# A fused decoder layer: output weights and one group of down weights split earlier, stored in HBM and read back

## The chip, the cores and the metric

The kernel runs on one core of a Trainium2 chip. Its engines are TensorE (PE, matmuls; PEld is its weight load), VectorE (DVE), ScalarE (ACT), GpSimd (POOL) and SyncE (SP, which here only issues DMAs). Each engine works through its own queue in order, and waits on semaphores for the others. SP, ACT and POOL each issue DMAs. SBUF holds the working tiles, PSUM the eight banks into which matmuls accumulate, and HBM the rest.

The metric is the device time of one execution in microseconds, as the median over runs.

## The reference

One step of a decoder layer on 1024 prompt tokens and 64 decode tokens (8 sequences of 8), all in float32. An RMS norm and one input projection feed two mixers, retention (8 heads) and sliding-window attention (8 query heads, 2 key/value heads). Their outputs are concatenated, projected by `w_out`, and added to the input; a squared-ReLU MLP of four times the width follows.

```python
hn = rms_norm(x, norm_mix_gain)
proj = hn @ w_in
...
o_r = rms_norm(o_r).reshape(b, t, RET_WIDTH) * jax.nn.silu(g_r)
...
h = x + jnp.concatenate([o_r, o_s], axis=-1) @ w_out
hf = rms_norm(h, norm_ffn_gain)
h = h + jnp.square(jax.nn.relu(hf @ w_up)) @ w_down
return h, new_ret, new_k, new_v
```

Here x has 1088 rows of 1024, `w_out` is 1024 x 1024, `w_up` 1024 x 4096 and `w_down` 4096 x 1024.

## The kernel before

**Split products.** Every large product is made of three matmuls in a fast float32 form (`mm3`, L174 to L177). Each operand is the sum of a high part, which is the value cast to that form, and a low part, which is what the cast left out; the three products are high x high, low x high and high x low. So each weight and each activation has to be split before use: one cast on ACT (L791) and one subtraction on DVE (L792), together `halve`. `wsplit` (L794) does that for a weight tile of 128 x 512, giving a tile of 128 x 2 x 512 (high and low). In `wload` (L66), for the input projection, the same is done at L80 and L82.

**The front** (L86 to L529). x is loaded and normalised, and the first two blocks of q columns are projected for the window attention (`proj_q`, L265). The loop at L307 then goes over nine token tiles, `proj_tok` giving k and v of the window attention, with a short chain over ACT, DVE and POOL for each tile. Before this loop its weights `wkv` are loaded; the second q block's weights `wq1` are loaded after it (L341). Then eight blocks of window attention follow (`swa_block`, L378). Their scores are in tiles of tag "s" (three buffers of 128 x 4 x 256) and their transposed probabilities in tiles of tag "pt" (two buffers of 128 x 2 x 512). PE fills the gaps of that chain with projections for retention.

**Retention and output projection** (L509 to L1089). The output projection starts while retention still runs: `out_early` for the first half of the tokens (s = 0), then `out_parts` for the second (s = 1). For each s, each pair of feature blocks m and each mixer ("a" attention, "r" retention), `wo_pair` (L819) loads half rows of two blocks of `w_out` into a raw tile and splits them in two `wsplit`s. So each half of each block of `w_out` is loaded and split twice, once for each s: 16 loads and 32 splits.

**Up** (L1098 to L1200). Sixteen blocks `up(fp)` of 256 hidden columns each. The product is done by a Strassen-like scheme with seven products in place of eight quarter products; the activations' combinations are in `ops`, and `left` (L1036) gives the seven weight tiles of a block one by one: some straight from the raw quarters (products 1, 2, 4), the others from sums on POOL (`comb`). The squared results go to HBM as `u_d`, seven combinations for each block. `first_down` loads and splits operands of the first products of down while the last block runs.

**Down** (L1206 to L1276). The sixteen blocks f are taken in five groups of 2, 4, 4, 4 and 2; in each group the seven products in the order `DOWN` = 1, 6, 7, 4, 5, 3, 2. For a product i of a group, each f's weight tile comes from its generator `left` (L1236), the activations `ur` are loaded from `u_d` (L1246) and split (`uh`, `ul`, L1248), and PE accumulates over f into eight banks (4 row blocks m, 2 halves s). A result is copied out of its bank by ACT the first time (L1264, `copied`) and added by DVE afterwards (L1267, `added`). New banks are taken at products 1, 5 and 2. Weight tiles have the tags "wa" and "wb", four buffers each.

**Order.** The program gives an order of emission; a planner with a timing model then sets the order of each engine's queue. `tc.issue_after(x)` puts what is emitted under it behind instruction x. Buffers of a tag go round: a tile waits until the last reader of the buffer's previous tile is done.

Of the kernel before, what the change touches and what calls it, by code (L numbers as in the profile page):

```python
# [11 lines left out]
F32 = mybir.dt.float32  # L12
F32R = mybir.dt.float32r
AF = mybir.ActivationFunctionType
ALU = mybir.AluOpType
# [5 lines left out]
P = 128  # L21
# [15 lines left out]
def hymba_layer(ctx: ExitStack, tc: tile.TileContext, a: dict, o: dict):  # L37
    nc = tc.nc
# [22 lines left out]
    def cload(name):  # L61
        t_ = const.tile(list(a[name].shape), F32, name="c_" + name)
        nc.sync.dma_start(t_, a[name])
        return t_

    def wload(src, kk, name, lo_eng="p", parts=2, after=()):  # L66
        hi = ring.tile([P, 2048], F32R, tag="whi", name=name + "_hi")
        lo = ring.tile([P, 2048], F32R, tag="wlo", name=name + "_lo")
        n = 2048 // parts
        after = list(after)  # L70
        for h in range(2):
            raw = ring.tile([P, 1024], F32, tag="raw", name=f"{name}_raw{h}", bufs=3)
            for q in range(0, 1024, n):
                nc.sync.dma_start(raw[:, q : q + n], src[:, h * 1024 + q : h * 1024 + q + n])
                if after:
                    load_x(*after.pop(0))
            for q in range(0, 1024, n):
                h_, l_ = (v[:, h * 1024 + q : h * 1024 + q + n] for v in (hi, lo))
                r_ = raw[:, q : q + n]
                nc.scalar.copy(h_, r_)  # L80
                eng = nc.vector if lo_eng[(2 * h + q // n) % len(lo_eng)] == "v" else nc.gpsimd
                eng.tensor_tensor(l_, r_, h_.bitcast(F32), ALU.subtract)  # L82
        return hi.rearrange("p (k n) -> p k n", k=kk), lo.rearrange("p (k n) -> p k n", k=kk)
# [44 lines left out]
    g_d = scratch.tile([P, 4, T], F32, name="g_d")  # L128
    ms_hi_d = scratch.tile([P, 4, T], F32, name="ms_hi_d")
    ms_lo_d = scratch.tile([P, 4, T], F32, name="ms_lo_d")  # L130
    y_d = scratch.tile([P, 4, 4, 2, Q], F32, name="y_d")
    u_d = [scratch.tile([P, 2, 2, 7, Q], F32, name=f"u_d{g}") for g in range(8)]

    def rsqrt_inplace(ap, n):
# [168 lines left out]
    spread(rst, rsb)  # L303


    w = wload(a["w_in"][2], 8, "wkv", "v")
    for t in range(9):  # L307
        off, c, r0 = tok_tile(t)
        rt = rst[:, t : t + 1]
        ps = proj_tok(t, w, psA.tile([P, 512], F32, tag="mm", name="pst"))  # L310
        sq = sp.tile([P, 128], F32, tag="hsq", name="hsq")
        nc.scalar.activation(sq, ps[:, :128], AF.Square, scale=rt)
        r = sp.tile([P, 2], F32, tag="hr", name="hr")
        nc.vector.tensor_reduce(r, sq.rearrange("p (h d) -> p h d", h=2), AX.X, ALU.add)
        nc.vector.tensor_scalar(r, r, 1.0 / 64.0, EPS, ALU.mult, ALU.add)
        rsqrt_inplace(r, 2)
        nc.vector.tensor_scalar(r, r, rt, None, ALU.mult)
        kn = sp.tile([P, 128], F32, tag="kn", name="kn")
        nc.vector.tensor_tensor(
            kn.rearrange("p (h d) -> p h d", h=2), ps[:, :128].rearrange("p (h d) -> p h d", h=2),  # L320
            r.unsqueeze(2).broadcast_to([P, 2, 64]), ALU.mult,
        )
        pt = psB.tile([P, 512], F32, tag="t2", name="ptk")[:, :128]
        nc.tensor.transpose(pt, kn, ident)
        if t < 8:
            cols = slice(t * 128, t * 128 + 128)
            for kv in range(2):
                p_ = slice(kv * 64, kv * 64 + 64)
                for d_ in (p_, slice(64 - kv * 64, 128 - kv * 64)):
                    nc.scalar.activation(kh2[kv][d_, cols], pt[p_], AF.Copy, scale=qkg[p_, 1:2])  # L330
                    nc.vector.scalar_tensor_tensor(
                        kl2[kv][d_, cols], pt[p_], qkg[p_, 1:2], kh2[kv][p_, cols].bitcast(F32), ALU.mult, ALU.subtract
                    )
            nc.vector.tensor_scalar(vs[:, t, :], ps[:, 128:256], rt, None, ALU.mult)
        if t == 7:
            nc.vector.tensor_scalar(k8[:, 0:128], pt, qkg[:, 1:2], None, ALU.mult)
        if t == 8:
            nc.vector.tensor_scalar(k8[:, 128:192], pt[:, 64:128], qkg[:, 1:2], None, ALU.mult)
            nc.vector.tensor_scalar(v8, ps[64:128, 128:256], rt[64:128], None, ALU.mult)

    proj_q(1, wload(a["w_in"][1], 8, "wq1", "v"))  # L341
    nc.sync.dma_start(o["kp"], k8[:, 0:128])
    nc.sync.dma_start(o["vp"], vs[:, 7, :])
    nc.sync.dma_start(o["kc"][:, :, 120:128], k8[:, 128:192].rearrange("p (b i) -> p b i", b=8))
# [473 lines left out]

    def wo_pair(s, m, half):  # L819

        raw = mw.tile([P, 1024], F32, tag="raw", name=f"wo{half}{s}_{m}_raw", bufs=3)
        c0 = 512 * (half == "a")
        nc.sync.dma_start(
            raw.rearrange("p (m n) -> p m n", m=2), a["w_out"][m : m + 2, :, c0 : c0 + 512].rearrange("m p n -> p m n")
        )
        for i in range(2):
            yield wsplit(raw[:, i * 512 : i * 512 + 512], "wa", f"wo{half}{s}_{m + i}", nc.vector)

    def out_half(s, half, ps, h, w, first, last):
        for k in range(4):  # L830
# [113 lines left out]
    qbh, qbl, kh, kl = split_space([ring.tile([P, 1024], F32R, tag="raw", name=f"qk{i}", bufs=3) for i in range(3)])  # L944
    for i, x in enumerate("hl"):
        mix[0, "r" + x] = slot(6 + i, F32R, "mixr" + x)[:, : 8 * Q].rearrange("p (k h n) -> p k h n", k=4, h=2)
    held, mxr, mxrx = {}, None, ExitStack()
    for t in range(5):
        if t == 0:
            for _ in range(2):  # L950
# [82 lines left out]
                for x in "hl"  # L1033
            ]

    def left(order, src, name, lo_eng, raw_tag="raw", raw_pool=None, s_tag="S", s_pool=None, tags=("wa", "wb"), raws=None, sums=None):  # L1036

        r1, r2 = raws or (
            rawload(src[:, i * 1024 : i * 1024 + 1024], f"{name}_r{i + 1}", raw_tag, raw_pool) for i in range(2)
# [8 lines left out]
        for n, i in enumerate(order):  # L1048
            if i in (5, 6) and 5 not in have:
                comb(5, a21, a22, ALU.add)  # L1050
                comb(6, have[5], a11, ALU.subtract)
            if i == 7:
                comb(7, a11, a21, ALU.subtract)
            if i == 3:
                comb(3, a12, have[6], ALU.subtract)
            yield wsplit(have[i], tags[n % len(tags)], f"{name}_w{i}", lo_eng)

    late = lambda: bank("pso")
# [137 lines left out]
        return lambda: halve(u_hi, u_lo, u_raw, nc.vector)  # L1196

    split6 = []
    for fp in range(16):
        up(fp)  # L1200
    opx.close()
    ux.close()

# [19 lines left out]
    for g, (f0, nf) in enumerate(((0, 2), (2, 4), (6, 4), (10, 4), (14, 2))):  # L1223
        gens = []
        for f in range(nf):
            own = ("rawb", dn, "Sb", dn) if f else ("raw", mw, "S", mid)
            gens.append(left(
                DOWN, a["w_down"][f0 + f], f"wd{f0 + f}", nc.vector, *own, tags=("wb" if f % 2 else "wa",),
                raws=raws1 if (g, f) == (0, 1) else None, sums=sums1 if (g, f) == (0, 1) else None))
        banks = {}  # L1230
        for i in DOWN:
            ws = []
            for f, gen in enumerate(gens):
                behind = copied[(6, 6, 7, 4)[f] if g == 1 else 4] if g in (1, 2) and i == 1 else None
                with tc.issue_after(behind) if behind else ExitStack():
                    ws.append(next(gen))  # L1236
            if g == 0 and i in begun:
# [6 lines left out]
            for f in () if g == 0 and i in begun else range(0, nf, 2):  # L1244
                if g or i in (3, 2):
                    nc.sync.dma_start(ur[:, f : f + 2], u_d[(f0 + f) // 2][:, :, :, RIGHT[i], :])  # L1246
                with tc.issue_after(copied[{4: 6, 5: 7}[i]]) if g == 0 and i in (4, 5) else ExitStack():
                    halve(uu[0][:, f : f + 2], uu[1][:, f : f + 2], ur[:, f : f + 2], nc.vector)  # L1248
            q_ = INTO[i]
            if q_ not in accs:  # L1250
                accs[q_] = dn.tile([P, 4, 2, Q], F32, tag=f"a{q_}", name=f"a{q_}")
# [147 lines left out]
```

## Time and profile before

| | us |
|---|---|
| median of 3 runs | 1189.44 |
| lowest, highest | 1187.9, 1189.73 |
| profiled execution | 1188.43 |
| its span | 1186.7 |

The page of the profile gives, for the span, the busy shares of the engines, the span in 40 slices, the DMA queues, the chain that ended last and the costliest groups of instructions. Of the chain, 81% is on PE, 6% on DVE, 5% on DMA, 3% on issue and 2% each on ACT and POOL. The granted clock of PE was full throughout. DMAs moved 169.44 MB, 143 GB/s in the mean.

| stage, by the first and last start of its matmuls | from, us |
|---|---|
| k and v of the window attention (`pst<-wkv`) | 31.9 to 73.3 |
| v of retention (`pst<-wv`) | 285.5 to 367.5 |
| output projection (`pso`) | 373.1 to 489.9 |

How to read it: a group of instructions has its line, engine, operation and tiles, then its count, its busy time and the mean length of one, and last how long its engine had stood idle just before, and for whom. The line is often that of a helper, so the tiles tell the stage. A matmul's end is modelled and the next one starts before it, so PE can show no idle time where it starts fewer matmuls than it could.

### The profile page before, as it was taken

How to read it: one execution, taken by the hardware profiler on the slowest of the kernel's cores; microseconds unless marked ns; L12 is line 12 of the kernel's file. 1: busy time of each engine (PE TensorE's matmuls, PEld its weight loads, DVE VectorE, ACT ScalarE, POOL GpSimd, SP SyncE). 2: the span in 40 equal slices, each digit the busy share in tenths (PEclk: the TensorE clock that was granted, in tenths of full speed). 3: DMA queues.
4: the chain of work that ended last, by engine and by line, in shares of the span. 5: the costliest groups of instructions: out<-in, count | busy, mean ns of one | idle time of the engine just before them, and what ended most of it. 6: DMA issues, size and time to landing. Idle time of an engine off the chain costs nothing.

```text
span 1186.7 us, 23488 instructions
## 1 busy us (share of the span) xinstructions
PE 1169.6 (99%) x9405; PEld 1123.5 (95%) x9405; DVE 839.1 (71%) x1546; ACT 513.8 (43%) x1055; POOL 494.2 (42%) x393
## 2 busy tenths in 40 slices
PE   8999999999999999999999999999999999999998
PEld 7999988989778899999999999999989999999998
DVE  7556868632257769887766667666788787888676
ACT  8343544553334347644444444444642333333231
POOL 0125333332255542467666666566383142053000
PEclk9999999999999999999999999999999999999999
DMA  7221235333525555343444434444685456443225
GB/s 247 73 62 68 93 102 166 104 115 98 180 74 168 181 183 156 113 156 133 141 151 148 144 130 141 151 148 157 236 290 157 148 169 203 143 155 104 76 59 187
DMA packets 102277, 169.44 MB, mean 143 GB/s; under 512 B 12000, under 2 KB 68256, under 8 KB 101912
## 3 DMA queue, kind: packets, MB, share of 16 engines
q1 hardware_dynamic: 88807, 123.80, 31.5%
q10 hardware_dynamic: 10800, 35.23, 9.3%
q0 software_dynamic: 2560, 8.91, 2.3%
q8 instruction: 74, 1.21, 0.4%
q14 instruction: 36, 0.29, 0.1%
HBM read 114.30 MB, written 53.61 MB: 142 GB/s over the span
## 4 chain that ended last, share of the span: by engine, by line
PE 81%; DVE 6%; DMA 5%; issue 3%; ACT 2%; POOL 2%; SPq 0%; ACTq 0%; DVEq 0%; POOLq 0%
PE psd L176 9%; PE psd L177 9%; PE psd L175 9%; PE psx L175 5%; PE psx L177 5%; PE psx L176 5%; PE psz L175 2%; PE psz L177 2%; PE psz L176 2%; PE pst L175 2%; PE pst L176 2%; PE pst L177 2%; PE psf L175 2%; PE psf L177 2%; PE psf L176 2%
## 5 line engine op out<-in xcount | busy, mean ns | idle before, releaser
L175 PE MATMUL psd<-uh,wd_w 128*128 128x272 f32 x896 | 258.4, 288 | 3.2 <-DVE a L1267 2.4
L176 PE MATMUL psd<-uh,wd_w 128*128 128x272 f32 x896 | 259.3, 289 | 0.0
L177 PE MATMUL psd<-ul,wd_w 128*128 128x272 f32 x896 | 257.9, 288 | 0.7 <-DVE ul L792 0.7
L175 PEld LDWEIGHTS psd<-uh,wd_w 128*128 128x128 f32 x896 | 169.1, 189 | 4.3 <-DVE a L1267 3.4
L177 PEld LDWEIGHTS psd<-ul,wd_w 128*128 128x128 f32 x896 | 168.7, 188 | 0.9 <-DVE ul L792 0.9
L176 PEld LDWEIGHTS psd<-uh,wd_w 128*128 128x128 f32 x896 | 168.4, 188 | 0.0
L1267 DVE TENSOR_TENSOR a<-a,psd 128x272 f32<-128x272 f32 x248 | 101.9, 432 | 48.9 <-PE psd L177 48.8
L792 DVE TENSOR_TENSOR wu_w<-wu_s,wu_w 128x512 fp32r<-128x512 f32 x64 | 61.9, 971 | 49.8 <-ACT wu_w L791 49.2
L791 ACT CAST wd_w<-wd_s 128x512 fp32r<-128x512 f32 x64 | 37.5, 621 | 119.0 <-PE psd L177 107.2
L792 DVE TENSOR_TENSOR ul<-ur,uh 128x1088 fp32r<-128x1088 f32 x56 | 84.0, 1527 | 4.1 <-ACT uh L791 4.1
L1120 DVE SCALAR_TENSOR_TENSOR m<-m,rsf 128x272 f32<-128x272 f32 x96 | 72.9, 760 | 3.2 <-ACT rsf L914 0.5
L175 PE MATMUL psx<-op_1h,wu_w 128*128 128x272 f32 x256 | 74.3, 290 | 0.4 <-ACT m L1136 0.4
L177 PE MATMUL psx<-op_1l,wu_w 128*128 128x272 f32 x256 | 74.1, 289 | 0.0
L175 PE MATMUL psx<-op_0h,wu_w 128*128 128x272 f32 x256 | 74.1, 290 | 0.0
L177 PE MATMUL psx<-op_0l,wu_w 128*128 128x272 f32 x256 | 74.1, 289 | 0.0
L176 PE MATMUL psx<-op_1h,wu_w 128*128 128x272 f32 x256 | 73.7, 288 | 0.0
L176 PE MATMUL psx<-op_0h,wu_w 128*128 128x272 f32 x256 | 73.7, 288 | 0.0
L365 POOL TENSOR_TENSOR sp<-sp,ssp 128x1024 f32<-128x1024 f32 (+1 forms) x16 | 28.6, 1787 | 88.4 <-DVE ssp L364 60.1
L791 ACT CAST uh<-ur 128x1088 fp32r<-128x1088 f32 x56 | 59.7, 1101 | 12.7 <-PE psd L176 9.1
L175 PE MATMUL psf<-hnh,wqk_hi 128*128 128x384 f32 (+1 forms) x192 | 63.5, 331 | 0.2 <-DVE qkst L517 0.2
L177 PE MATMUL psf<-hnl,wqk_hi 128*128 128x384 f32 (+1 forms) x192 | 63.2, 329 | 0.0
L176 PE MATMUL psf<-hnh,wqk_lo 128*128 128x384 f32 (+1 forms) x192 | 62.8, 327 | 0.0
(343 smaller groups left out, 3619.4 us busy)
## 6 DMA issues: line engine op xcount, KB each, us to landing
ur<-u_d SPq DMA_DIRECT2D x53, 544.0 KB, 5.2
u_d<-r4t SPq DMA_DIRECT2D x32, 544.0 KB, 4.6
wu_r<-in_w_up ACTq DMA_DIRECT2D x32, 512.0 KB, 4.4
wd_r<-in_w_down ACTq DMA_DIRECT2D x30, 512.0 KB, 6.5
u_d<-r3t SPq DMA_DIRECT2D x32, 408.0 KB, 2.9
y<-in_xY POOLq DMA_DIRECT2D x16, 272.0 KB, 3.5
y_d<-y POOLq DMA_DIRECT2D x16, 272.0 KB, 3.2
yt<-y_d SPq DMA_DIRECT2D x16, 272.0 KB, 2.9
```

Source lines behind the costliest of these rows:

```text
L175: nc.tensor.matmul(ps, lh, rh, start=first, stop=False, skip_group_check=more)
L176: nc.tensor.matmul(ps, ll, rh, start=False, stop=False, skip_group_check=more)
L177: return nc.tensor.matmul(ps, lh, rl, start=False, stop=last, skip_group_check=more)
L365: nc.gpsimd.tensor_tensor(s, s, ss.unsqueeze(2).broadcast_to([P, 4, n]), ALU.mult)
L791: nc.scalar.copy(hi, src)
L792: lo_eng.tensor_tensor(lo, src, hi.bitcast(F32), ALU.subtract)
L1120: nc.vector.scalar_tensor_tensor(t_, src, 0.0, rsf[:, s, h, :], ALU.max, ALU.mult)
L1267: added[i] = nc.vector.tensor_tensor(to, to, ps, ALU.add).ins
```

## The change

Two things are done earlier and once, and two small ones are reordered.

1. **Output weights.** In the loop over the nine token tiles in the front, after each tile but the last, one of eight blocks of `w_out` is loaded (behind the last raw load of `wq1`, which now is loaded ahead of the loop), split in two halves, and stored in HBM as `wo_d`, high and low. The raw tile borrows tag "s", the split tile tag "pt". Later `wo_pair` only loads the split tile: 32 loads in place of 16 loads and 32 splits. Of each seven such tiles four have the tag "wa" and three the tag "raw" (three buffers).
2. **Down, second group.** During up blocks 3 to 10, the weights of product 1 for f = 2 to 5 are loaded in halves of 256 columns, split, and stored as `wd_d`, through one tile of a new pool. In the second group, `left` loads this tile in place of splitting it. The raw loads of the block stay.
3. **One cast.** In the first group, product 5's weight splits are put behind ACT's last bank copy of product 6.
4. **Halves.** In the first group, the activations of product 7 are split in two pieces, one for each f.

```diff
+    wo_d = [scratch.tile([P, 2, 1024], F32, name=f"wo_d{m}") for m in range(8)]
+    wd_d = {f: scratch.tile([P, 2, 512], F32, name=f"wd_d{f}") for f in range(2, 6)}
...
-    w = wload(a["w_in"][2], 8, "wkv", "v")
+    def split_out(m):
+        raw = sp.tile([P, 4, 256], F32, tag="s", name=f"wo_raw{m}", bufs=3).rearrange("p k n -> p (k n)")
+        with tc.issue_after(raw_loads[-1].ins):
+            nc.sync.dma_start(raw, a["w_out"][m])
+        for c in (slice(0, 512), slice(512, 1024)):
+            w = sp.tile([P, 2, 512], F32R, tag="pt", name=f"wo_hl{m}")
+            nc.scalar.copy(w[:, 0, :], raw[:, c])
+            nc.vector.tensor_tensor(w[:, 1, :], raw[:, c], w[:, 0, :].bitcast(F32), ALU.subtract)
+            nc.sync.dma_start(wo_d[m][:, :, c], w.bitcast(F32))
+
+    w, w_q1 = (wload(a["w_in"][i], 8, n, "v") for i, n in ((2, "wkv"), (1, "wq1")))
     for t in range(9):
+        if t:
+            split_out(t - 1)
...
-    proj_q(1, wload(a["w_in"][1], 8, "wq1", "v"))
+    proj_q(1, w_q1)
...
     def wo_pair(s, m, half):
 
-        raw = mw.tile([P, 1024], F32, tag="raw", name=f"wo{half}{s}_{m}_raw", bufs=3)
         c0 = 512 * (half == "a")
-        nc.sync.dma_start(
-            raw.rearrange("p (m n) -> p m n", m=2), a["w_out"][m : m + 2, :, c0 : c0 + 512].rearrange("m p n -> p m n")
-        )
         for i in range(2):
-            yield wsplit(raw[:, i * 512 : i * 512 + 512], "wa", f"wo{half}{s}_{m + i}", nc.vector)
+            tag, bufs = ("raw", 3) if len(w_loads) % 7 > 3 else ("wa", 4)
+            w = mw.tile([P, 2, 512], F32R, tag=tag, name=f"wo{half}{s}_{m + i}", bufs=bufs)
+            w_loads.append(nc.sync.dma_start(w.bitcast(F32), wo_d[m + i][:, :, c0 : c0 + 512]))
+            yield w
...
+            if i == 1 and stored is not None:
+                w = (mid if tags[0] == "wb" else mw).tile([P, 2, 512], F32R, tag=tags[0], name=f"{name}_w1", bufs=4)
+                nc.sync.dma_start(w.bitcast(F32), stored)
+                yield w
+                continue
             yield wsplit(have[i], tags[n % len(tags)], f"{name}_w{i}", lo_eng)
...
+    pre = opx.enter_context(pool("pre", side="left"))
+
+    def split_down(f, c):
+        w = pre.tile([P, 2, 256], F32R, tag="pw", name=f"pw{f}_{c}")
+        nc.sync.dma_start(w[:, 1, :].bitcast(F32), a["w_down"][f][:, c : c + 256])
+        nc.scalar.copy(w[:, 0, :], w[:, 1, :].bitcast(F32))
+        nc.vector.tensor_tensor(w[:, 1, :], w[:, 1, :].bitcast(F32), w[:, 0, :].bitcast(F32), ALU.subtract)
+        nc.sync.dma_start(wd_d[f][:, :, c : c + 256], w.bitcast(F32))
+
     for fp in range(16):
         up(fp)
+        if 2 < fp < 11:
+            split_down(2 + (fp - 3) // 2, 256 * ((fp - 3) % 2))
...
+                stored=wd_d[f0 + f] if g == 1 else None))
...
+                if (g, i) == (0, 5):
+                    behind = copied[6]
                 with tc.issue_after(behind) if behind else ExitStack():
                     ws.append(next(gen))
...
-                    halve(uu[0][:, f : f + 2], uu[1][:, f : f + 2], ur[:, f : f + 2], nc.vector)
+                    n = 1 if (g, i) == (0, 7) else 2
+                    for j in range(f, f + 2, n):
+                        halve(uu[0][:, j : j + n], uu[1][:, j : j + n], ur[:, j : j + n], nc.vector)
```

More of the change, by code (lines that the diff above doesn't have):

```diff
@@ L64, in cload @@
         return t_
+    raw_loads = []
     def wload(src, kk, name, lo_eng="p", parts=2, after=()):
@@ L73, in wload @@
             for q in range(0, 1024, n):
-                nc.sync.dma_start(raw[:, q : q + n], src[:, h * 1024 + q : h * 1024 + q + n])
+                raw_loads.append(nc.sync.dma_start(raw[:, q : q + n], src[:, h * 1024 + q : h * 1024 + q + n]))
                 if after:
@@ L946, in hymba_layer @@
         mix[0, "r" + x] = slot(6 + i, F32R, "mixr" + x)[:, : 8 * Q].rearrange("p (k h n) -> p k h n", k=4, h=2)
-    held, mxr, mxrx = {}, None, ExitStack()
+    held, mxr, mxrx, w_loads = {}, None, ExitStack(), []
     for t in range(5):
@@ L1034, in operand_tiles, with left @@
             ]
-    def left(order, src, name, lo_eng, raw_tag="raw", raw_pool=None, s_tag="S", s_pool=None, tags=("wa", "wb"), raws=None, sums=None):
+    def left(order, src, name, lo_eng, raw_tag="raw", raw_pool=None, s_tag="S", s_pool=None, tags=("wa", "wb"), raws=None, sums=None, stored=None):
         r1, r2 = raws or (
@@ L1228, in hymba_layer @@
                 DOWN, a["w_down"][f0 + f], f"wd{f0 + f}", nc.vector, *own, tags=("wb" if f % 2 else "wa",),
-                raws=raws1 if (g, f) == (0, 1) else None, sums=sums1 if (g, f) == (0, 1) else None))
+                raws=raws1 if (g, f) == (0, 1) else None, sums=sums1 if (g, f) == (0, 1) else None,
+                stored=wd_d[f0 + f] if g == 1 else None))
         banks = {}
```

## The prediction

> **What bounds the kernel now.** I read the busy shares first, then the busy time in stretches of 20 us, then what TensorE (PE) waited for, and last the neighbouring engines in the stretches where it waited.
>
> ```profile
> PE 1169.6 (99%) x9405; PEld 1123.5 (95%) x9405; DVE 839.1 (71%) x1546; ACT 513.8 (43%) x1055; POOL 494.2 (42%) x393
> ```
>
> PE is busy for all but 17.1 us of the 1186.7 us span, and the change takes no matmul away, so it can win only what PE loses between matmuls. The stretches (columns: length; busy time and instructions of PE, PEld, DVE, ACT, POOL; granted clock; DMA share; GB/s) say where that is:
>
> ```profile
> 380.00:400.00 20.00, 18.64 (x215) 17.34 (x214) 14.95 (x37) 5.63 (x10) 10.30 (x8) 1.00 0.66 216
> 400.00:420.00 20.00, 18.66 (x182) 17.91 (x181) 15.97 (x33) 10.00 (x17) 9.88 (x11) 1.00 0.42 127
> ...
> 840.00:860.00 20.00, 18.60 (x146) 18.18 (x145) 14.48 (x18) 14.80 (x37) 6.92 (x6) 1.00 0.78 276
> 860.00:880.00 20.00, 18.68 (x146) 18.25 (x146) 16.78 (x21) 11.52 (x20) 19.19 (x11) 1.00 1.04 358
> 880.00:900.00 20.00, 18.82 (x148) 18.38 (x147) 17.96 (x31) 5.36 (x8) 10.29 (x7) 1.00 0.43 133
> 900.00:920.00 20.00, 20.00 (x162) 20.00 (x161) 16.25 (x26) 6.17 (x9) 6.43 (x4) 1.00 0.58 182
> ```
>
> Two places matter: 1.36 + 1.34 = 2.7 us while the output projection is interleaved with retention (380 to 420), and the start of down (840 to 900). There all matmuls have one shape, so I count them: 162 in a full stretch (20 us / 162 = 0.123 us each), but 146, 146 and 148, that is 16 + 16 + 14 = 46 missing, 5.7 us. That is more than the 3.9 us of idle time, because a short gap hides behind the modelled end of the matmul before it. The other 17.1 - 2.7 - 3.9 = 10.5 us of idle time are the first loads, the drain and single gaps, out of the change's reach but for one gap named next.
>
> Who PE waited for, from 835 to 890 us and then from 375 to 540 us:
>
> ```profile
> PE psd L175 <- DVE a L1267: 2.4, 3, 1.2
> PE psd L175 <- ACT a L1264: 0.7, 1, 0.7
> PE psd L177 <- DVE ul L792: 0.7, 1, 0.7
> ```
>
> ```profile
> PE pm L771 <- DVE mtr L619: 1.3, 1, 1.3
> PE rsr L175 <- ACT qkb L709: 1.2, 1, 1.2
> PE psz L176 <- DVE wu_w L792: 0.9, 1, 0.9
> ```
>
> **The change part by part. Down, the second group's first weights.** PE's largest wait is for VectorE's (DVE) bank adds (`a`, L1267). Stretches of 6 us, and DVE's own timeline, show what stood ahead of them:
>
> ```profile
> 860.00:866.00 6.00, 6.00 (x50) 6.00 (x50) 4.59 (x4) 4.21 (x10) 5.42 (x4) 1.00 1.03 380
> 866.00:872.00 6.00, 6.00 (x50) 6.00 (x49) 4.18 (x6) 4.00 (x6) 5.92 (x4) 1.00 1.09 356
> 872.00:878.00 6.00, 5.88 (x47) 5.66 (x46) 6.00 (x10) 2.85 (x5) 5.84 (x5) 1.00 0.98 333
> 878.00:884.00 6.00, 3.62 (x24) 2.96 (x24) 6.00 (x9) 0.46 (x1) 6.00 (x4) 1.00 0.74 233
> ```
>
> ```profile
> 872.48 1.43 DVE L792 TENSOR_TENSOR wd_w<-wd_r,wd_w 128x512 fp32r<-128x512 f32 x1
> ...
> 875.23 1.62 DVE L792 TENSOR_TENSOR wd_w<-wd_r,wd_w 128x512 fp32r<-128x512 f32 x1
> ...
> 881.71 1.41 DVE L792 TENSOR_TENSOR wd_w<-wd_r,wd_w 128x512 fp32r<-128x512 f32 x1
> 883.04 1.47 DVE L1267 TENSOR_TENSOR a<-a,psd 128x272 f32<-128x272 f32 x4
> ```
>
> From 872 to 884 DVE is full (6.00 of 6.00, twice), and PE does 47 and 24 matmuls where it did 50: 29 missing x 0.123 = 3.6 us. Three operations in that queue split the very weights that the change reads back stored (product 1 takes its weights straight from the raw tile, `wd_r`): 1.43 + 1.62 + 1.41 = 4.5 us of DVE, more than the 3.6 us lost. Their ACT casts go too, off the path. The adds then come that much earlier. Bounds: 0 (other splits move up ahead of the adds) to 3.6; I take **3.0**, near the upper end, since DVE has less to do whatever the order. What is late next is the same group's activations (`ur`, `uh`, `ul`).
>
> What comes in: four loads of 512 KB on SP's queue (128 x 2 x 512 floats each). All raw loads stay, since the other products need them. That is 2.1 MB where the DMA share is 1.03 and 1.09, so 2.1 MB / 356 GB/s = 5.9 us of the engines' time. Each load waits for its tile to come free, and behind it on SP stand the loads of the activations. After 878 the share falls to 0.74, and in 880 to 900 to 0.43, so the debt is paid within that stretch; PE reaches the second group only after the adds at 883.04. I cost it at nothing; without that cover it costs up to 3 us (rivals).
>
> **Down, the first group: one cast, and halves.** ACT's timeline, then DVE's:
>
> ```profile
> 844.79 0.62 ACT L791 CAST wd_w<-wd_s 128x512 fp32r<-128x512 f32 x1 [1.42 <-PE psd L177]
> ...
> 845.38 2.41 ACT L1264 COPY a<-psd 128x272 f32<-128x272 f32 x8
> ...
> 850.68 1.10 ACT L791 CAST uh<-ur 128x1088 fp32r<-128x1088 f32 x1 [1.05 <-DMA ur<-u_d]
> ```
>
> ```profile
> 851.82 1.29 DVE L792 TENSOR_TENSOR ul<-ur,uh 128x1088 fp32r<-128x1088 f32 x1 [1.15 <-ACT uh L791]
> ```
>
> The cast at 844.79 (product 5's weights) stands ahead of the eight bank copies for one of which PE waits 0.7 us. Put behind product 6's copies, it costs the path nothing (products 7 and 4 still lie before product 5) and PE starts up to 0.6 us earlier. Then PE waits 0.7 us for `ul` of product 7: the chain is 1.10 + 1.29 = 2.39 us after the landing of `ur`. In halves, the first half of the activations is there after about half of that, some 1.2 us (estimate; each piece's fixed cost makes it rather 1.4). PE would go on 1.0 us earlier than now, at about 852.1 instead of 853.1. This includes the 0.6 us, because the landing does not move. I take **1.0**; bounds 0 (if the landing moves, or the pieces come out of order) and 2.0 (the 16 matmuls missing in 840 to 860).
>
> **Output weights.** In the interleaved stage these go:
>
> ```profile
> L792 DVE TENSOR_TENSOR wor<-wor_raw,wor 128x512 fp32r<-128x512 f32 x16 | 12.1, 756 | 4.4 <-ACT wor L791 4.3
> ...
> L792 DVE TENSOR_TENSOR woa<-woa_raw,woa 128x512 fp32r<-128x512 f32 x16 | 11.5, 720 | 0.8 <-ACT woa L791 0.6
> ```
>
> That is 12.1 + 11.5 = 23.6 us of DVE and 32 casts on ACT. But of the three waits above only `pm` <- `mtr` is DVE's, and there a power on GpSimd stands ahead of it; `rsr` <- `qkb` waits for the load of `qt`, and `wu_w` for GpSimd's sums. So most of the 23.6 us is hidden. SP's queue gets 32 loads of 512 KB in place of 16: 8.4 MB more in some 110 us, 76 GB/s. The tightest stretch is the one in which `qt` is loaded:
>
> ```profile
> 390.00:400.00 10.00, 9.96 (x124) 9.11 (x123) 7.35 (x23) 1.93 (x4) 6.22 (x6) 1.00 0.90 301
> ```
>
> 301 + 76 = 377 GB/s, about the most that any row here shows (380), so `qt` can be later by 1 us or two. Bounds: +3.6 (all of 2.7 + 0.9 gone) and -3 (`qt` two microseconds later, another load one). I take **+1.0**, nearer to the middle: DVE's relief is certain, its use is not.
>
> **The front.** Added: eight loads (512 KB), 16 casts, 16 subtractions and 16 stores (512 KB) on SP, between the k/v tiles:
>
> ```profile
> 46.00:74.00 28.00, 28.00 (x290) 27.43 (x289) 19.58 (x72) 13.42 (x37) 8.05 (x11) 1.00 0.17 48
> 74.00:90.00 16.00, 16.00 (x98) 15.74 (x96) 5.66 (x18) 5.62 (x13) 5.41 (x3) 1.00 0.25 79
> ```
>
> ```profile
> L792 DVE TENSOR_TENSOR wu_w<-wu_s,wu_w 128x512 fp32r<-128x512 f32 x64 | 61.9, 971 | 49.8 <-ACT wu_w L791 49.2
> ```
>
> ```profile
> u_d<-r4t SPq DMA_DIRECT2D x32, 544.0 KB, 4.6
> ```
>
> ```profile
> 101.76 0.61 DVE L401 SCALAR_TENSOR_TENSOR sp<-dtab,nsl,scp 128x128 f32<-128x128 f32 x2
> ```
>
> At 0.97 us a subtraction, DVE gets 16 x 0.97 = 15.5 us; between 46 and 90 it has 8.4 + 10.3 = 18.8 us free (ACT: 25.0). A split tile is held for its cast, subtraction and store, 0.6 + 1.0 + 4.6 = 6.2 us; two buffers, 16 tiles: 8 x 6.2 = 50 us, so from about 35 (after the first loads) to 85. The window attention takes its first score tile at 101.76, so the shared buffers are free in time. DMA has room (0.17 and 0.25). PE covers the slower k/v tiles with the q projection whose weights now come first. Still, every k/v step can stand behind a subtraction, so I take **-0.8**; bounds +0.4 and -8 (the slow rival).
>
> **During up**: eight small loads, casts, subtractions and stores, one set in each of eight of the sixteen blocks, on engines that PE did not wait for there: 0, at worst -1 if a store on SP holds up those of `u_d`.
>
> **Sum**: 3.0 + 1.0 + 1.0 - 0.8 = 4.2 us off. The profiled execution took 1188.43 (span 1186.7 and 1.7 around it) and the median is 1189.44, 1.0 above; I take 4.2 from the median: **1185.2 us**.
>
> **Rivals.**
>
> *All of it is won.* 3.6 + 2.0 + 3.6 = 9.2, less 0.8 in the front: 8.4 off, 1181.0. For it: DVE and ACT lose over 40 us of work where PE waits. Against: two of those waits hang on GpSimd and a load.
>
> *The DMA engines take the place of DVE.* From 854 to 878 they are full. The 5.9 us of added transfers stand beside the activations of the second group, which need a cast and subtraction after landing; in the output stage `qt` comes later. Down then wins 1.1 instead of 4.0, output loses 0.5, front 0.3: 0.3 off, 1189.1. Against: the raw loads of the next group, in the same queue of work, are early and can give way. The Trainium skill ("DMA: Bandwidth & Descriptors", section "Issuing engines are not separate DMA queues") says that transfers issued from SP, ACT and POOL run on the same 16 engines and interleave. By that rule the loads on SP gain nothing from the raw loads being on ACT's queue, and the sum would be this rival's.
>
> *The front becomes DVE's* (slower). If a subtraction takes over 18.8 / 16 = 1.17 us, as the 1.43 to 1.62 us of the rows at 872 to 881 do beside a busy GpSimd, the stretch from 46 to 90 is full, k/v ends late and the window attention after it. At 1.6 us they cost 25.6 us, 6.8 over; PE has nothing else to do once the q projection is used up: 6.8 less 4.2 + 0.8 won elsewhere, 1.8 over, and with the tiles' own waits up to 8: 1191.2 to 1192.4, I say 1192. Against: GpSimd is busy there for 13.5 of 44 us only.
>
> *The order does not follow.* A planner sets each queue's order; freed time may be filled by other splits ahead of the adds, and the waits stay: 1189.4.
>
> **How the numbers follow.** Forecast 0.50 (own range 1183 to 1187), all won 0.16, DMA 0.16, order 0.08, front 0.10. A measurement of this kernel tells 0.2% (2.4 us) from no change: faster is below 1187.1, slower above 1191.8. Faster: 0.50 + 0.16 = 0.66; same: 0.16 + 0.08 = 0.24; slower: 0.10. The range goes from 1180.5, the case where all is won, to 1190.8; past these lies the front rival and little else.
>
> **What would show it.** Right: from 840 to 900 at least 40 of the 46 matmuls back; no wait of PE for `a` L1267 of over 0.3 us; the stored loads landed before PE reaches the second group; `ul` of product 7 in two pieces, PE's wait for it at 0.2 or less. DVE in 380 to 500 less by 20 us or more, with PE's waits for `mtr` and `wu_w` shorter. Wrong: PE below 19.5 of 20 anywhere between 40 and 300; first scores later than 110; PE waiting for stored weights or `qkb` for over 2 us.

## The result and the profile after

| | before | after |
|---|---|---|
| median, us | 1189.44 (5 runs) | 1219.09 (5 runs) |
| lowest, highest | 1187.9, 1190.03 | 1211.63, 1221.53 |
| profiled execution | 1188.43 | 1211.63 |
| its span | 1186.7 | 1209.9 |

The ratio after to before is 1.0237 (95% interval 1.0217 to 1.0257): the change makes the kernel 2.4% slower. The prediction, 1185.2 us and at most 1190.8, had the sign wrong; it gave slower a chance of 0.10.

To see where the time went, I cut both spans at the first starts of three groups of matmuls (the tile views of `wv`'s products, `psx` and `psd`):

| stretch | before | after | longer by | the prediction's term |
|---|---|---|---|---|
| start of the span to the first `pst<-wv` (the front) | 285.6 | 306.3 | 20.7 | 0.8 |
| to the first `psx` (retention, output projection) | 210.4 | 210.6 | 0.2 | -1.0 |
| to the first `psd` (up) | 336.8 | 343.1 | 6.3 | 0 |
| to the end of the span (down) | 353.9 | 349.9 | -4.0 | -4.0 |

The four differences make up the 23.2 us between the spans. The profiled execution after is the fastest of its five, so this accounts for 23.2 of the 29.65 us between the medians. Down did what was forecast; two stretches that were costed at next to nothing lost 27.0 us. Two lines of the page after, the busy times and the shares of the chain that ended last:

```profile
PE 1175.5 (97%) x9405; PEld 1128.7 (93%) x9405; DVE 827.4 (68%) x1535; ACT 506.7 (42%) x1046; POOL 486.0 (40%) x393
...
PE 72%; DMA 11%; DVE 9%; ACT 4%; issue 2%; POOL 1%; SPq 0%; ACTq 0%; DVEq 0%; POOLq 0%
```

DVE and ACT have less work than before (839.1 and 513.8 us then), and yet PE is idle for 1209.9 - 1175.5 = 34.4 us where it was idle for 17.1. In the chain that ended last, DMA has 11% where it had 5%. So look for waits on transfers.

**The front.** Stretches of 20 us, before and then after, with the columns of the prediction's table (length; busy time and count of PE, PEld, DVE, ACT, POOL; granted clock; DMA share; GB/s):

```profile
40.00:60.00 20.00, 20.00 (x259) 19.28 (x258) 14.58 (x48) 10.12 (x24) 4.57 (x6) 1.00 0.19 55
60.00:80.00 20.00, 20.00 (x155) 19.96 (x155) 13.47 (x47) 10.98 (x27) 8.70 (x8) 1.00 0.17 59
```

```profile
40.00:60.00 20.00, 17.38 (x233) 15.81 (x232) 13.86 (x43) 10.15 (x22) 5.00 (x6) 1.00 0.72 235
60.00:80.00 20.00, 11.26 (x82) 11.02 (x80) 7.25 (x23) 5.46 (x15) 1.39 (x2) 0.74 0.89 133
```

In 60 to 80 every engine does about half of what it did or less, DVE and ACT too, although their work was added here. None of them is the bound: all stand still together. What PE waited for, over the whole span, largest first:

```profile
PE ptk L340 <- DVE kn L335: 8.7, 1, 8.7
PE psx L179 <- ACT m L1156: 5.1, 3, 3.7
...
PE psd L179 <- ACT a L1300: 0.9, 1, 0.9
...
PE psd L179 <- DVE a L1303: 0.4, 1, 0.4
```

The largest is one wait of 8.7 us for `kn`, a step of the chain of k and v. ACT's timeline shows what stood ahead of that chain (start, length, engine, line, tiles; in brackets the idle time before it):

```profile
72.44 0.62 ACT L316 CAST wo_hl<-wo_raw 128x512 fp32r<-128x512 f32 x1 [8.81 <-issue]
73.08 0.36 ACT L346 ACTIVATE kk<-ptk,c_qkg 64x128 fp32r<-64x128 f32 x1
73.47 0.37 ACT L328 ACTIVATE hsq<-pst,rst 128x128 f32<-128x128 f32 x1
```

A cast of the new split stands for 8.81 us at the head of ACT's queue, and `kk` and `hsq` of the k/v chain run right behind it, in order. The releaser is given as "issue", that is, none was found; the view of the tile `wo_hl` says for whom its instructions wait:

```profile
L317 DVE TENSOR_TENSOR wo_hl<-wo_raw,wo_hl x16: 678/692/2891, 34.8 to 93.7; 128x512 fp32r<-128x512 f32 x16
...
  DMA wo_d<-wo_hl: 17.2, 7
  issue: 8.8, 1
...
DMA to landing us min/median/max: 3.0/4.1/12.6
```

A store of `wo_d` takes 4.1 us in the median and 12.6 at most, and only when it has landed is its buffer free for the next cast. The view gives ACT seven waits for such a store, 17.2 us in all; the 8.8 us for which it names no releaser are an eighth, as the next views show, so it is 26.0 us together. The critical chain between 55 and 80 (start, length, piece) and SP's timeline show what lay in the way:

```profile
58.44 13.37 DMA r_d<-rst
...
72.31 5.80 DMA wo_d<-wo_hl
```

```profile
58.00 0.39 SPq L172 DMA_DIRECT2D r_d<-rst  x1
58.44 0.71 SPq L173 DMA_DIRECT2D r_d<-rst  x1
59.74 0.52 SPq L318 DMA_DIRECT2D wo_d<-wo_hl  x1
71.88 0.33 SPq L174 DMA_DIRECT2D rsb<-r_d  x1
72.31 0.51 SPq L318 DMA_DIRECT2D wo_d<-wo_hl  x1
```

`r_d<-rst` stores the 1088 norm factors, 4 bytes each, in two stores of 1024 and of 64 values, which take 13.6 and 13.4 us. A `wo_d` store issued behind them at 59.74 is the one of 12.6 us: 59.74 + 12.6 = 72.3, and the cast starts at 72.44. SP itself stands still from 60.3 to 71.88, since `rsb<-r_d` reads back what was stored. That is a second way to be late, and the critical chain takes this one: the next split was ready at 61.3 (its subtraction on DVE runs from 60.60 for 0.68 us), but its store stood behind `rsb<-r_d` in SP's queue until 72.31, landed at 78.11, and the cast that needed its buffer started at 78.19, after 4.10 us of waiting. No run separates the two ways. In short stretches:

```profile
58.00:62.00 4.00, 4.00 (x36) 4.00 (x35) 2.88 (x8) 2.53 (x6) 0.63 (x1) 1.00 1.35 188
62.00:66.00 4.00, 4.00 (x35) 3.94 (x33) 1.91 (x7) 1.51 (x5) 0.70 (x1) 1.00 1.10 16
66.00:70.00 4.00, 0.14 (x2) 0.00 (x0) 0.00 (x0) 0.00 (x0) 0.00 (x0) 0.76 0.66 50
70.00:74.00 4.00, 0.00 (x0) 0.00 (x0) 0.88 (x2) 1.51 (x4) 0.00 (x0) 0.50 0.42 92
74.00:78.00 4.00, 3.12 (x15) 3.12 (x16) 1.47 (x7) 0.08 (x1) 0.70 (x1) 0.50 1.00 283
```

From 62 to 66 the DMA engines are counted full (1.10) and move 16 GB/s. From 66 to 74 PE does two matmuls, and the granted clock falls to 0.50 and is still there when PE goes on (74 to 78).

**Up.** Two lines of ACT's timeline, and then four of the issues on SP (the first, the second, and the tenth and eleventh from 510 on):

```profile
537.62 0.41 ACT L1224 CAST pw<-pw 128x256 fp32r<-128x256 f32 x1 [4.49 <-DMA pw<-in_w_down]
537.93 0.38 ACT L1156 COPY m<-psx 128x272 f32<-128x272 f32 x1
```

```profile
510.95 0.34 SPq L1223 DMA_DIRECT2D pw<-in_w_down  x1
515.50 0.56 SPq L1226 DMA_DIRECT2D wd_d<-pw  x1
...
546.71 0.51 SPq L1226 DMA_DIRECT2D wd_d<-pw  x1
547.62 1.02 SPq L1173 DMA_DIRECT2D u_d<-r3t  x2
```

The program emits these splits behind up's blocks 3 to 10. In the queue the first load stands at 510.95, before up's first product at 516.9, and five of eight loads go ahead of the first store of `u_d`. There is one `pw` tile, so it goes load, cast, subtraction, store, landing, next load, one after the other, and each cast waits in ACT's queue ahead of the bank copies `m`, for which PE then waits the 5.1 us above.

**Down.** The stretches where the prediction counted 46 matmuls missing, after:

```profile
860.00:880.00 20.00, 20.00 (x161) 20.00 (x160) 15.15 (x21) 12.98 (x32) 9.84 (x8) 1.00 0.58 204
880.00:900.00 20.00, 18.71 (x147) 18.28 (x146) 12.96 (x15) 13.74 (x28) 12.89 (x8) 1.00 1.05 368
900.00:920.00 20.00, 20.00 (x161) 20.00 (x160) 20.00 (x30) 5.42 (x8) 14.83 (x10) 1.00 0.80 285
```

Down starts later by 27 us (860.0 against 832.8), so 860 to 920 answers to the old 833 to 893. From 867.2 on, which answers to 840 to 900, the counts are 162, 147 and 161. So one stretch lacks 15 (a full one has 161 or 162), where three lacked 46. PE's waits for `a` are 0.4 us for DVE's, where they were 2.4, and 0.9 for ACT's, where they were 0.7.

### The profile page after: what moved, and what is told of

Same layout as the page of the kernel before. It is cut to its first block, busy times and chain, and to the rows that moved or that the text cites. A ratio compares the mean times of both kernels' runs of the same rounds, so it can differ in the third digit from the quotient of the medians.

```text
span 1209.9 us, 23594 instructions
## 1 busy us (share of the span) xinstructions
PE 1175.5 (97%) x9405; PEld 1128.7 (93%) x9405; DVE 827.4 (68%) x1535; ACT 506.7 (42%) x1046; POOL 486.0 (40%) x393
## 4 chain that ended last, share of the span: by engine, by line
PE 72%; DMA 11%; DVE 9%; ACT 4%; issue 2%; POOL 1%; SPq 0%; ACTq 0%; DVEq 0%; POOLq 0%
PE psd L180 9%; PE psd L179 9%; PE psd L181 9%; PE psx L179 5%; PE psx L181 5%; PE psx L180 5%; PE psz L179 2%; PE psz L181 2%; PE psz L180 2%; DMA wo_d<-wo_hl 2%; PE psf L179 2%; PE psf L181 2%; PE psf L180 2%; DMA wd_d<-pw 1%; PE pst L179 1%
## 5 line engine op out<-in xcount | busy, mean ns | idle before, releaser
L808 DVE TENSOR_TENSOR ul<-ur,uh 128x1088 fp32r<-128x1088 f32 (+1 forms) x57 | 82.3, 1471 | 6.4 <-ACT uh L807 6.4
L1140 DVE SCALAR_TENSOR_TENSOR m<-m,rsf 128x272 f32<-128x272 f32 x96 | 69.4, 723 | 2.6
L807 ACT CAST uh<-ur 128x1088 fp32r<-128x1088 f32 (+1 forms) x57 | 59.7, 1084 | 15.1 <-PE psd L180 10.1
```

The costliest lines, as they stand in the source:

```text
L807: nc.scalar.copy(hi, src)
L808: lo_eng.tensor_tensor(lo, src, hi.bitcast(F32), ALU.subtract)
L1140: nc.vector.scalar_tensor_tensor(t_, src, 0.0, rsf[:, s, h, :], ALU.max, ALU.mult)
```

## The experiments

My theory after this comparison: the front pays for the *stores* of the split tiles, because each tile is held until its store lands and the next cast then blocks ACT's queue; and up pays because the splits through one tile run far ahead of their place. The rivals: the added work on DVE and ACT, or the added load traffic, costs the front by itself; the slower stretch of up only follows from the later front; and down's gain is not from the parts that I named.

### The parts one by one

`d1_front_only` has the output weights alone, `d2_down_only` the down parts alone (stored weights, one cast, halves), `d4_small_only` only the one cast and the halves. `d3_down_gated` is `d2` with the splits held at their place in up:

```diff
-                nc.sync.dma_start(u_d[fp // 2][:, fp % 2, s, 3:, :], rb[s])
+                last_store[0] = nc.sync.dma_start(u_d[fp // 2][:, fp % 2, s, 3:, :], rb[s]).ins
...
-            split_down(2 + (fp - 3) // 2, 256 * ((fp - 3) % 2))
+            with tc.issue_after(last_store[0]):
+                split_down(2 + (fp - 3) // 2, 256 * ((fp - 3) % 2))
```

> The kernel before with the output weights stored in the front, and nothing of down. By the start of the matmuls of each stage, the changed kernel lost 20.7 us up to the start of retention's v, 0.2 us more up to the first up product, 6.3 us more up to the first down product, and won 4.0 us from there to the end. If the parts are independent: 20.9 us over the kernel before, 1208 to 1220 (the changed kernel's own runs spread by 10 us), and up begins and ends as before. Rival: the loss at the start of up comes from the output weights too (their tiles hold the raw buffers that up's first weights need): then 27 us over.

> The kernel before with the down parts alone (stored weights, one cast, halves). Independent parts: 6.3 us lost at the start of up, where the splits for down run early through their single tile, and 4.0 us won in down: 2.3 us over the kernel before, 1191.7. Rival (the output weights cause the loss at the start of up): 4.0 us won, 1185.4.

> As the down parts alone, but each of the eight loads for the stored weights is issued behind the last store of the up block that it belongs to, so that load, cast, subtraction and store happen in blocks 3 to 10. Theory (early splits stall ACT and DVE behind a store that is still under way): the loss in up goes, 4.0 us are won, 1185.4 (ratio 0.9966). Rival (the added work costs wherever it is): like the down parts alone, 1191.7.

> The kernel before with the one cast behind the bank copies and product 7 in halves, no stored weights. By the prediction's terms 1.0 of the 4.0 us won in down: 1188.4 (ratio 0.9992), and the waits for the bank adds stay at 2.4 us. Rival: the two small edits bring all of it by starting the first group earlier: 1185.4.

Measured, beside a median of 1189.26 of the kernel before; the last three columns are the lengths of the stretches of the table above:

| kernel | median, us | ratio (95%) | front | up | down |
|---|---|---|---|---|---|
| before (first table) | | | 285.6 | 336.8 | 353.9 |
| `d1_front_only` | 1211.17 | 1.0183 (1.0164 to 1.0203) | 306.5 | 338.4 | 354.8 |
| `d2_down_only` | 1192.46 | 1.0025 (1.0015 to 1.0034) | 284.7 | 342.8 | 350.0 |
| `d3_down_gated` | 1186.44 | 0.9977 (0.9967 to 0.9987) | 286.2 | 337.2 | 350.5 |
| `d4_small_only` | 1188.27 | 0.9991 (0.9982 to 1.0000) | 284.8 | 336.8 | 353.1 |

`d1` and `d4` came out as expected, `d2` 0.8 us above and `d3` 1.0 above. The output weights alone lengthen the front by 20.9 us and up by 1.6; the down parts alone lengthen up by 6.0 us with no late front. So up's loss is not a consequence of the front's. Holding the splits back takes up from 342.8 to 337.2 and keeps down's gain, and the two medians, 6.0 us apart, have intervals that lie far from each other.

The rival in the expectation of `d1` has something for it, though. Of the kernels without a split in up, those without the stored output weights have 336.3 to 336.8 there (before, `d4`, and `f1` and `h1` below), those with them 335.8 (`f2`), 338.4 (`d1`) and 340.7 to 341.4 (`f3`, `h2`, `f4`). In `d1` PE waits 1.8 us for one of up's first weights (`wu_w`), in `h2` 3.0, before 0.9. ACT issues the first raw load of up's weights 24 us ahead of up in the kernel before (472.1) and 17 to 18 us ahead in these five. That would fit tiles that hold the raw buffers longer, but `f2` loads as late and loses nothing, and no run tests it alone: the cause stays open.

The view of `pw` in `d3_down_gated`, and a stretch at the start of up in `d2_down_only` and then in `d3_down_gated` (up starts at 498.2 and 497.2):

```profile
L1211 SPq DMA_DIRECT2D pw<-in_w_down x8: 356/383/1971, 595.4 to 744.4; - x8
...
  DMA pw<-in_w_down: 19.7, 8
```

```profile
520.00:540.00 20.00, 18.82 (x150) 18.60 (x149) 17.77 (x27) 8.32 (x20) 13.41 (x11) 1.00 0.58 188
```

```profile
520.00:540.00 20.00, 19.61 (x156) 19.39 (x155) 18.63 (x28) 9.68 (x22) 11.28 (x10) 1.00 0.54 178
```

Note that ACT still waits 19.7 us for these loads, more than the 15.7 us that the same view shows for the changed kernel and the 12.8 us in `d2`. But the loads now lie from 595 to 744, one in each block, and PE is busy for 219.8 of 220 us from 560 to 780. In 500 to 560 it is busy for 58.9 us, as in the kernel before (58.7), where `d2` has 53.9. The sum of a wait says little; what is queued behind it says what it costs. This kernel is faster than the kernel before by 0.23% (2.8 us), and than the changed one.

### The front: work, stores, or the small store in their way

`f1_no_stores` keeps the front's loads, casts and subtractions and drops the stores; the output stage is that of before:

```diff
-            nc.sync.dma_start(wo_d[m][:, :, c], w.bitcast(F32))
```

`f2_packed_r` is `d1` with the norm factors turned on PE and stored as nine rows in place of 1088 single values:

```diff
-        nc.sync.dma_start(r_d[0:1024].rearrange("(t p) -> p t", p=128), rst[:, :8])
-        nc.sync.dma_start(r_d[1024:1088].rearrange("(p t) -> p t", t=1), rst[64:128, 8:9])
...
+        nc.tensor.transpose(pt, rst, ident)
...
+        nc.vector.tensor_copy(rr[:9], pt)
+        nc.sync.dma_start(r_d[0:1024].rearrange("(t p) -> t p", p=128), rr[:8])
+        nc.sync.dma_start(r_d[1024:1088].unsqueeze(0), rr[8:9, 64:128])
```

`f3_four_tiles` is `d1` with every second split in two tiles of other tags, so that four splits are in flight instead of two:

```diff
-            w = sp.tile([P, 2, 512], F32R, tag="pt", name=f"wo_hl{m}")
...
+        pairs = [(w[:, 0, :], w[:, 1, :])]
+        pairs.append(tuple(sp.tile([P, 512], F32R, tag="m" + x, name=f"wo_{x}{m}") for x in "hl"))
...
```

`f4_both` has both.

> The kernel before plus the front's eight loads, 16 casts and 16 subtractions, without the 16 stores; the output stage loads and splits its weights itself, as before. This leaves out only the storing of the split tiles. Wait theory (the casts stand in ACT's queue until the store of the tile before has landed): without stores a split tile is free as soon as its subtraction is done, so the front costs 0 to 3 us, 1189 to 1192. Work theory (10 us more on ACT and 11 to 15 us more on DVE, between the k/v chains): the front costs 10 us or more, at least 1199.

> The output weights in the front as in the first of these runs (1211.2), but the 1088 factors of the norm, which go to HBM as 4-byte packets from 128 partitions, are transposed on TensorE first and stored as nine rows. If that store, which takes 12.5 us to land and holds the DMA engines, makes the one long stall (8.9 us of PE, a split tile's store under way for 12.6 us): 9 to 12 us less, 1199 to 1202. Rival (two buffers and stores of 4 to 6 us are enough to stall the queue): at most 3 us less, 1208 to 1211.

> The output weights in the front, with every second split tile in two tiles of the window attention's result tags in place of tag pt, so four split tiles are under way in place of two (the second of each block is stored by two DMAs). Wait theory: a cast waits for the store of four tiles ago; 8 to 15 us less than 1211.2, 1196 to 1203. Work theory: no change, 1211.

> Both of these, packed factors and four split tiles. Wait theory: the front's cost is nearly gone, 1190 to 1195; what stays over 1189.3 is the work itself and the output stage. Work theory: 1209 or more.

Measured beside 1189.38 us of the kernel before (front: to the first `pst<-wv`, and what it has over 285.6; last, for how long ACT's casts of the new splits waited for a store, from its waits between 30 and 110):

| kernel | median, us | ratio (95%) | front | more than before | casts waited |
|---|---|---|---|---|---|
| `d1_front_only` (above) | 1211.17 | 1.0183 (1.0164 to 1.0203) | 306.5 | 20.9 | 22.5 |
| `f1_no_stores` | 1192.69 | 1.0027 (1.0017 to 1.0036) | 288.5 | 2.9 | 0 |
| `f2_packed_r` | 1204.36 | 1.0117 (1.0098 to 1.0136) | 298.2 | 12.6 | 14.4 |
| `f3_four_tiles` | 1205.41 | 1.0128 (1.0111 to 1.0145) | 296.4 | 10.8 | 8.2 |
| `f4_both` | 1198.41 | 1.0074 (1.0046 to 1.0101) | 293.1 | 7.5 | 5.9 |

(The 22.5 us of `d1` are 14.6 in six waits and one of 7.9 without a releaser, like the 8.8 above.) The same loads, casts and subtractions without stores cost 2.9 us of the 20.9 of `d1`; the other 18.0 come with the stores. The front goes with the waits of the casts, so the wait theory holds, but its sizes did not: `f1` came out 0.7 us above its range, `f2` between its range and its rival's, `f3` and `f4` 2.4 and 3.4 us above theirs. Of the front, packing `r_d` takes 8.3 us off, two more tiles 10.1, both together 13.4, as if they partly cured the same wait. By the medians it is 6.9, 5.9 and 12.9, which simply add; so how far the two overlap stays open. The view of `r_d` in `f2_packed_r`, and that of `wo_hl`:

```profile
DMA to landing us min/median/max: 5.3/5.3/5.3
```

```profile
  DMA wo_d<-wo_hl: 14.4, 7
...
DMA to landing us min/median/max: 3.0/4.3/7.1
```

The single long store is gone (at most 7.1 us here, 12.0 in `d1`), but seven casts still wait, 14.4 us in all: even a store of ordinary length holds one of two tiles. That is the half that more tiles mend, and `f4_both` still has 7.5, with 5.9 us of such waits left. The 4.6 us between it and `f1` were not taken apart further.

### The controls

`h1_before_packed_r` is the kernel before with `f2`'s edit. `h2_free_weights` asks what the output stage would gain if the splits cost nothing at all: the 32 loads from `wo_d` as in the change, but no split anywhere; `wo_d` is filled by 16 copies from HBM to HBM in the front.

```diff
+    with tc.issue_after(raw_loads[-1].ins):
+        for m in range(8):
+            for j in range(2):
+                nc.sync.dma_start(wo_d[m][:, j, :], a["w_out"][m])
```

`h3_gated_stored` is `d3` without the one cast and the halves; `h4_change_again` is the changed kernel once more.

> The kernel before, with only the norm's factors transposed on TensorE and stored as nine rows. A control for the packed run: if the 4-byte store hurts only what waits for a transfer beside it, nothing changes here, 1189 (within 2 us), since in the kernel before no engine waits for a DMA between 54 and 67. Rival: the packed form is worth 8 us by itself, 1181.

> The kernel before with the output stage's 32 loads and without its 32 splits, as in the change, but without the front's casts and subtractions: `wo_d` is filled from HBM to HBM, with the raw weights in both places, so the splitting of the output weights is left out altogether. It prices the gain in the output stage: from the first matmul of retention's v to the first of up, 210.4 us before. By the prediction 1.0 us less (at most 3.6); by the stages of the runs so far (209.0 to 212.7 with the stored weights) 0, within 2.

> The stored down weights alone, their splits held back to blocks 3 to 10; without the one cast and without the halves. By the prediction's term 3.0 us won in down, 1186.4. By the difference of the held-back run (2.8 won) and the two small edits (1.0): 1.8 won, 1187.6. If the parts need each other (the small edits only move the wait): under 1.5 won.

> The changed kernel itself, beside the others on one chip: output weights alone cost 21.9 and the down parts 3.2, together 25.1, so 1214.5 if nothing else is in it; the first measurement had 29.6 over.

Measured beside 1189.61 us:

| kernel | median, us | ratio (95%) | front | retention, output | up | down |
|---|---|---|---|---|---|---|
| `h1_before_packed_r` | 1191.71 | 1.0014 (1.0003 to 1.0025) | 287.1 | 211.8 | 336.3 | 354.7 |
| `h2_free_weights` | 1204.98 | 1.0126 (1.0098 to 1.0154) | 299.2 | 213.3 | 340.9 | 353.9 |
| `h3_gated_stored` | 1187.72 | 0.9990 (0.9980 to 1.0000) | 284.9 | 212.2 | 338.3 | 351.7 |
| `h4_change_again` | 1214.31 | 1.0212 (1.0198 to 1.0225) | 305.7 | 209.4 | 346.6 | 349.9 |

`h1`: in the kernel before, `r_d` takes 12.5 us too, and shortening it to 3.9 wins nothing (it loses 0.14%, 2.1 us, where none within 2 was expected). The small store is harmless there; in `d1`, where transfers with a waiter stand behind it, the same edit wins 6.9 us.

`h2`: 32 casts and 32 subtractions less, and the stage takes 213.3 us, 2.9 more than before, outside both expectations. Kernels that leave this stage as it was have 210.2 (`f1`) to 213.5 (`d2`), so there is no gain that could be told from their scatter. The profiled execution is one of the longest of its six, though (1209.13 us, the median is 1204.98). In the critical chain of `h2` the residual's store and load stand where DVE's splits had been thought to be:

```profile
439.60 5.66 DMA y_d<-y
...
452.88 7.13 DMA y<-in_xY
460.13 0.45 DVE y L845
```

The DMA issues of the stage show the same for the changed kernel: before (370 to 500), then after (390 to 520).

```profile
y_d<-y POOLq DMA_DIRECT2D x15, 272.0 KB, 3.3
...
kt<-kr_d SPq DMA_DIRECT2D x2, 256.0 KB, 4.6
qt<-qr_d SPq DMA_DIRECT2D x2, 256.0 KB, 7.3
```

```profile
y_d<-y POOLq DMA_DIRECT2D x16, 272.0 KB, 4.4
...
kt<-kr_d SPq DMA_DIRECT2D x2, 256.0 KB, 9.1
qt<-qr_d SPq DMA_DIRECT2D x2, 256.0 KB, 9.9
```

What DVE waited for, from the views of `y` from 370 to 525, before and then after:

```profile
  DMA y<-in_xY: 6.7, 6
```

```profile
  DMA y<-in_xY: 17.7, 6
```

Transfers that the stage waits for are slower beside the stored weights: `y_d` by 1.1 us, `qt` by 2.6, `kt` by 4.5. DVE, which has less to do, waits 11.0 us longer for the residual `y`, which comes back from HBM. `h2` loses 13.6 us in the front too, though nothing is split there: copies that nobody waits for stand among the loads that PE waits for (PE is busy 14.77 of 20 us in 40 to 60, at a DMA share of 0.84). I did not separate whether it is their traffic or their place in SP's queue.

`h3` against `d3` and `d4`: down gains 2.2 us by the stored weights alone, 0.8 by the small edits alone, 3.4 by both. Kernels without either have 353.7 to 356.5, 354.8 in the mean, and the kernel before lies low among them: against the mean the gains are 3.1, 1.7 and, over the four kernels with both, 4.7. The medians of the whole kernels give 1.9 (`h3`, as expected from the difference), 1.0 (`d4`) and 2.8 (`d3`). So these gains are good to a microsecond or two. `h4`: the median of the changed kernel is 1214.31 here and 1219.09 in the first measurement; `d1` and `d2` added to the kernel before make 1189.26 + 21.9 + 3.2 = 1214.4. The parts add up. Why the changed kernel's executions differ among themselves (1211.63 to 1221.53, where the kernel before stays within 1187.9 to 1190.03) a single profile cannot show, and it stays open; the mean granted clock on record is 0.994 for the one of 1211.63 us and 0.987 for the one of 1221.53.

## Why the prediction was wrong, step by step

Gains are positive here.

**The front, -0.8 forecast, -20.7 measured: the step that failed.** The prediction had worked out a split tile's time, 6.2 us, and 50 us for sixteen through two tiles; their subtractions start from 34.8 to 93.7, 59 us, so this was nearly of the right size. It then set only the *work* against the free time of DVE and ACT and let "PE covers the slower k/v tiles" stand for the rest. It did see that a k/v step can stand behind a subtraction, but not behind a cast that itself waits for a store: behind each such cast stand the k/v chain's own steps on ACT, behind these DVE's, and behind these PE. These waits, 22.5 us in `d1`, had no term. The work by itself (`f1`: 2.9) stayed inside the bounds given, the waits did not. Second, "DMA has room (0.17 and 0.25)" was read from a share, while the trace of before already held a store of 4 KB that took 12.5 us from issue to landing. Only SP's queue waited for it then (11.5 us, `rsb<-r_d`), no engine that computes did, and the prediction does not name it.

**The slow rival had the right place and the wrong mechanism.** It made DVE's subtractions the bound, from 1.17 us each. They took 0.69 in the median, less than the 0.97 forecast, and DVE was *less* busy than before in 60 to 80 (7.25 us against 13.47). So its price of at most 8 us, 1192, was a price for something that did not occur, and the range ended at 1190.8, short even of that. That the kernel came out slower is no credit to it.

**During up, 0 forecast, -6.3 measured: wrong.** The term took the program's order, "one set in each of eight of sixteen blocks", for the queue's order, while the fourth rival knew that the planner sets it. `d2` prices it alone at 6.0. The same work at the place assumed costs 0.4 (`d3`) to 1.5 (`h3`), near the 0 to -1 of the term. The 6.3 also holds what the output weights cost in up (1.6 in `d1`); measured again, the changed kernel has 9.8 there.

**Output weights, +1.0 forecast, -0.2 measured.** Inside its bounds. DVE did lose work (77.5 us in 400 to 520 after, 95.8 in 380 to 500 before, by the sums of the stretches: 18.3 less, the mark was 20). PE's waits for `mtr` and `wu_w` are gone from the changed kernel as marked, but it waits 1.7 us for `qkb` (1.2 before) and 1.3 for `y` (none before), and the reason named against the gain is what the traces show: `qt`, `kt` and `y_d` land later, and DVE waits for `y`. One pair of profiles is too little for 1 us: over the kernels that were profiled, the stage takes 211.6 us in the mean as it was (seven, 210.2 to 213.5) and 210.5 with the stored weights (six without `h2`, 209.0 to 212.7). But up takes that back: from retention's v to the start of down, the kernels without splits in up take 546.8 to 549.0 us without the stored weights and 547.4 to 554.2 with them. So no gain is shown, and if anything a loss. The rival with the DMA engines in DVE's place named what happens in this stage, and was wrong for down.

**Down, +4.0 forecast, +4.0 measured.** The mechanism was right: the four splits are gone from DVE's queue and the adds come earlier. That 4.0 met 4.0 is partly luck: the stored weights gave 2.2 (forecast 3.0), the small edits 0.8 (1.0), each measured alone in one profile, together 3.4 to 4.0, and 2.8 by the medians of `d3`. Of the marks set: about 30 of 46 matmuls came back (forecast 40), PE's wait for DVE's `a` fell from 2.4 to 0.4 (forecast 0.3) while that for ACT's stayed (0.9), the wait for `ul` is gone, and PE nowhere waits for a stored weight. In `d4` the first group's gain shows clearly: 840 to 860 is full, and the loss moves into 860 to 880.

```profile
840.00:860.00 20.00, 20.00 (x161) 20.00 (x160) 14.90 (x20) 15.87 (x40) 6.93 (x6) 1.00 0.81 285
860.00:880.00 20.00, 17.57 (x137) 17.08 (x136) 15.22 (x19) 11.20 (x20) 19.01 (x11) 1.00 1.02 353
```

Two of the three marks for "wrong" came true: PE below 19.5 of 20 between 40 and 300 (11.26), and the first score tile of the window attention came at 121.28 (mark: later than 110). The third did not: PE waited 1.7 us for `qkb` (mark: over 2).

## What to carry to other kernels

When a split is moved into a quiet stretch, cost not its work but its tile: the time from its first use to the landing of its store, times the number of splits over the number of tiles, and ask at each engine what stands in order behind an instruction that waits for such a tile. Work moved "into free time" needs a gate that holds it there: here the planner put it where its inputs were ready, 6 us dearer. And before adding a transfer with a waiter, search the stretch for transfers that take long and that no engine waits for yet.

## What was not expected of the hardware

- Two stores of 1024 and 64 values of 4 bytes (4.0 and 0.2 KB, one issued right behind the other) took 10.7 us (`h2`) to 13.6 us (after) each; as rows, nine in all, they took 3.9 (`h1`) to 5.3 (`f2`). The Trainium skill ("DMA: Bandwidth & Descriptors", section "Specifications") says that below 512 B an engine reads, modifies and writes; the runs show the price, and not which step takes it.
- Beside them, a 512 KB store took 12.6 us (after) to 13.6 us (`f3`), where the median of the changed kernel is 4.1; with the rows the longest was 7.1 (`f2`) and 7.9 (`f4`). The share of the DMA engines read 1.10 at 16 GB/s: a high share is not a high rate, and in the kernel before, the share was 0.00 from 58 to 66 while the same two stores were under way (the first issued at 54.5, landed 12.5 us later).
- After about 8 us without matmuls the granted clock was 0.50 for the next 3 us of work (74.9 to 78). The Trainium skill ("TensorE: Matmul & The Clock Gate", section "What's actually happening") gives half the clock after an idle window of about 3.4 us. The traces have the half, but not one such time: the last matmul before the gap starts at 65.9 both in the changed kernel and in `d1`. In stretches of 1 us, the clock of the first was full until 68 and 0.54 in 68 to 69, some 2 us later; that of `d1` was full until 71 and 0.66 in 71 to 72, some 5 us later.
